# Softmax times V: normalising bank by bank, with half of the last head's first bank on ScalarE and the very last store in three parts

## Chip, cores, metric

One core of a Trainium2 chip runs the whole problem as one program. The metric is the device time of one execution in microseconds (us); lower is better. All runs quoted here, the profiled ones too, are marked as fast in the record. A profile shows one run, and not always a median one: that of three_only took 1064.35 us (median 1064.08), that of bank_three 1064.14 (1063.76).

## The reference

```python
# scores: 8 x 12 x 1024 x 1024 fp32, v: 8 x 12 x 1024 x 64 fp32
def reference(scores, v):
    scores_max = np.max(scores, axis=-1, keepdims=True)
    attn = np.exp(scores - scores_max)
    attn = attn / (np.sum(attn, axis=-1, keepdims=True) + 1e-8)
    return np.matmul(attn, v).astype(np.float32)
```

There are 96 heads. The kernel reads 402.65 MB of scores, 25.17 MB of v, and writes 25.17 MB: 453 MB in all. It leaves the maximum out, takes the exponential, multiplies by v with a column of ones beside it, and divides by the sum that this column gives.

## The kernel before

A loop of 24 iterations takes a group of four heads (k = 0 to 3) each. A head is 8 blocks of 128 query rows (r = 0 to 7), here called rows. For each row ScalarE takes the exponential (two rows at once, except at a group's end), PE transposes the 128x1024 block in 8 matmuls, VectorE copies the result from PSUM to SBUF, and PE multiplies it in 8 matmuls, three rows behind (LAG). Four rows' products of 65 columns share one PSUM bank, so a head has bank 0 (rows 0 to 3) and bank 1.

```python
    # heads(n0): one group; 4 heads of 8 rows
            for r in range(R):
                ...                                   # exp -> p_nat (ScalarE)
                for c in range(C):
                    turned = nc.tensor.transpose(out=psT[:, c * P : (c + 1) * P], ...)
                    in_line(turned)
                copy = nc.vector.tensor_copy(out=pt[:], in_=psT[:])
                ...
                if k == AHEAD - 1 and r == R - 1:
                    normalise(k, st, 0, 1, copy)      # bank 0 of the last head
                ...
                pending.append((n0, k, r, pt, st))
                if len(pending) > LAG:
                    finish(pending.pop(0))            # 8 products of an earlier row
```

Even heads keep both banks in one tile and are normalised in one go at their end; odd heads are normalised bank by bank. W is 64, T is 2: one normalisation is a reciprocal and two products, one for each half t of the partitions.

```python
    psO_whole = ps_pool.tile([P, R // G, 512], FP32, name="psO_whole")
    psO_banks = buffers(ps_pool, R // G, [P, 1, 512], FP32, "psO")
    ...
    def normalise(k, st, first, last, behind=None):
        psO = psO_whole if k % 2 == 0 else psO_banks[first]
        ...
        inverse = nc.vector.reciprocal(out=recip, in_=psO[:, :, :, D : D + 1])
        for t in range(T):
            ...
            nc.vector.tensor_tensor(out=rows..., in0=psO[part, :, :, 0:D],
                                    in1=recip[part].to_broadcast(...), op=mult)
```

Two heads share an output tile and are stored together, 512 KB at a time. The very last store is cut in two by t. All loads and stores stand in one queue, issued by SyncE (SP).

The softmax here doesn't subtract the row's maximum and nothing guards it: scores larger than these inputs give would overflow.

Of the kernel before, what the change touches and what calls it, by code (L numbers as in the profile page):

```python
# [8 lines left out]
FP32 = mybir.dt.float32  # L9
# [5 lines left out]
def kernel(  # L15
# [6 lines left out]
    nc = tc.nc  # L22
    P = 128

    B, H, SQ, SK = scores.shape
    Bv, Hv, SKv, D = v.shape
# [3 lines left out]
    R = SQ // P  # L30
    C = SK // P
    M = D + 1
    EB = 2
    G = 4
    LAG = 3
    AHEAD = 4
# [3 lines left out]
    T = 2  # L40
# [10 lines left out]
    W = P // T  # L51
    out_bh = out.rearrange("b h (j x) d -> (b h j) (x d)", j=W)
# [3 lines left out]
    ps_pool = ctx.enter_context(tc.tile_pool(name="pspool", bufs=1, space=bass.MemoryType.PSUM))  # L56
# [6 lines left out]
        out=order16[:].rearrange("p (t j) -> p t j", t=T),  # L63
        in_=ident32[:].rearrange("p (j t) -> p t j", t=T),
# [3 lines left out]
    vones_bufs = []  # L68
# [7 lines left out]
    def buffers(pool, count, shape, dtype, name):  # L76
        return [pool.tile(shape, dtype, name=f"{name}{k}") for k in range(count)]
# [5 lines left out]
    out_bufs = buffers(sb_pool, 2, [P, T, R, D], FP32, "out_sb")  # L83
# [1 line left out]
    psT_bufs = buffers(ps_pool, 4, [P, SK], FP16, "psT")  # L85


    psO_whole = ps_pool.tile([P, R // G, 512], FP32, name="psO_whole")
    psO_banks = buffers(ps_pool, R // G, [P, 1, 512], FP32, "psO")
    turn = {}  # L90

    def take(bufs):
        k = turn.get(id(bufs), 0)
        turn[id(bufs)] = k + 1
        return bufs[k % len(bufs)]
# [5 lines left out]
    def after(a, b):  # L101

        tc.add_manual_dep(
            a.ins,
            b.ins.name,
            mybir.DependencyInfo(mybir.DependencyClass.NoSync, mybir.DependencyReason.DATA),
            reason="order",
        )

    def in_line(op):  # L110

        if line:
            after(op, line[-1])
        line.append(op)

    def queue(dma):

        if queued:
            after(dma, queued[-1])
        queued.append(dma)  # L120
# [1 line left out]
    def one(bh, n):  # L122
        return bh[bass.ds(n, 1)].rearrange("o p r d -> (o p) r d")

    def normalise(k, st, first, last, behind=None):

        psO = psO_whole if k % 2 == 0 else psO_banks[first]
        psO = psO[:, :, 0 : G * M].rearrange("p b (g m) -> p b g m", m=M)
        recip = st["recip"][:, first:last]
        inverse = nc.vector.reciprocal(out=recip, in_=psO[:, :, :, D : D + 1])  # L130
        if behind is not None:
            after(inverse, behind)
        h = k % T
        for t in range(T):
            part = slice(t * W, (t + 1) * W)
            rows = st["out_sb"][h * W : (h + 1) * W, t, first * G : last * G, :]
            nc.vector.tensor_tensor(  # L137
                out=rows.rearrange("j (b g) d -> j b g d", g=G),
                in0=psO[part, :, :, 0:D],
                in1=recip[part].to_broadcast([W, last - first, G, D]),  # L140
                op=mybir.AluOpType.mult,
            )

    def finish(u):

        n0, k, r, pt, st = u
        b, g = r // G, r % G
        if r == 0:
            st["recip"] = take(rc_bufs)
            st["out_sb"] = out_bufs[k // T]  # L150
        bank = psO_whole[:, b] if k % 2 == 0 else psO_banks[b][:, 0]
        for c in range(C):
            product = nc.tensor.matmul(  # L153
                out=bank[:, g * M : (g + 1) * M],
                lhsT=pt[:, c * P : (c + 1) * P],
                rhs=st["vones"][:, c, 0:M],
                start=(c == 0),
                stop=(c == C - 1),
            )
            in_line(product)  # L160
        if k % 2 == 1:
            if g == G - 1 and (b > 0 or k < AHEAD - 1):
                normalise(k, st, b, b + 1)
        elif r == R - 1:
            normalise(k, st, 0, R // G)
        if r == R - 1:
            spread_v(k)
            if k == T - 1:
                store(n0, 0)

    def store(n0, k, parts=1):

        rows = out_bh.rearrange("(m x) y -> m x y", x=P)
        size = T * R * D // parts
        for part in range(0, T * R * D, size):
            dma = nc.sync.dma_start(
                out=rows[bass.ds((n0 + k) // T, 1)].rearrange("o x y -> (o x) y")[
                    :, part : part + size
                ],
                in_=out_bufs[k // T][:].rearrange("x t r d -> x (t r d)")[:, part : part + size],  # L180
            )
            for other in stores:
                apart(dma, other)
                apart(other, dma)
            apart(dma, dma)
            stores.append(dma)
            queue(dma)
# [4 lines left out]
    def apart(a, b, reason="stores of two heads are disjoint"):  # L192
        tc.declare_no_dep(a.ins, b.ins, across_iterations=True, reason=reason)
# [11 lines left out]
    def load(k, n, parts=(R,), r=0, **cond):  # L205
        for rows in parts:
            queue(
                nc.sync.dma_start(  # L208
                    out=s_bufs[k][:, r : r + rows, :],
                    in_=one(sc_bh, n)[:, r : r + rows, :],  # L210
                    **cond,
                )
            )
            r += rows
# [11 lines left out]
    def spread_v(k):  # L226

        for s in range(S):
            nc.gpsimd.tensor_copy(  # L229
                out=vones_bufs[k][s * Q : (s + 1) * Q, :, 0:D].rearrange(  # L230
                    "i (h l) d -> i h l d", l=L
                ),
                in_=v_sb[k * Q : (k + 1) * Q, :, s],
            )
# [6 lines left out]
    def last(n0):  # L241


        before = queued[-1:]

        with tc.If(n0 < BH - 2 * AHEAD) as cmp:  # L246
            queued[:] = before
            load(AHEAD - 2, (n0 + (2 * AHEAD - 2)) % BH)
            load_v((n0 + 2 * AHEAD) % BH)
            load(AHEAD - 1, (n0 + (2 * AHEAD - 1)) % BH)  # L250
            store(n0, AHEAD - T)
        with cmp.Else():
            with tc.If(n0 < BH - AHEAD) as cmp2:
                queued[:] = before
                load(AHEAD - 2, BH - 2, (4, 4))
                load(AHEAD - 1, BH - 1, (3,))
                store(n0, AHEAD - T)
                load(AHEAD - 1, BH - 1, (2, 1, 1, 1), 3)
            with cmp2.Else():
                queued[:] = before  # L260
                store(n0, AHEAD - T, T)

    def heads(n0):

        for k in range(AHEAD):
            st = dict(vones=vones_bufs[k])
            for r in range(R):
                if r % EB == 0:
                    p_nat = take(p_bufs)
                    rows = 1 if k == AHEAD - 1 and r > 0 else EB  # L270
                    for g in range(0, EB, rows):
                        exp = nc.scalar.activation(  # L272
                            out=p_nat[:, g : g + rows, :].rearrange(
                                "p r (x v) -> p x r v", v=Q * L
                            ),
                            in_=s_bufs[k][:, r + g : r + g + rows, :].rearrange(
                                "p r (i x l) -> p x (r i) l", i=Q, l=L
                            ),
                            func=EXP,
                        )  # L280
                        rewrite(p_nat, exp)
                p_row = p_nat[:, r % EB, :].rearrange("p (h q l) -> p h l q", q=P, l=L)
                psT = take(psT_bufs)
                for c in range(C):
                    turned = nc.tensor.transpose(  # L285
                        out=psT[:, c * P : (c + 1) * P],
                        in_=p_row[:, c // L, c % L, :],
                        identity=order16[:],
                    )
                    in_line(turned)  # L290
                pt = take(pt_bufs)
                copy = nc.vector.tensor_copy(out=pt[:], in_=psT[:])  # L292
                rewrite(pt, copy)
                if k == AHEAD - 1 and r == R - 1:

                    normalise(k, st, 0, 1, copy)
                if r == R - 1:
                    load_next(k, n0)
                pending.append((n0, k, r, pt, st))
                if len(pending) > LAG:  # L300
                    finish(pending.pop(0))
        while pending:
            finish(pending.pop(0))
        last(n0)

    assert BH % AHEAD == 0 and BH >= 2 * AHEAD and SK == Q * S * C
# [40 lines left out]
```

## Time and profile before

| | |
|---|---|
| time, median of 3 (later of 6) runs | 1064.0 us (1063.86 to 1064.33) |
| span of the profiled run | 1061.8 us |
| DMA engines busy | full in 39 of 40 slices |
| last scores landed | 1052.04 |
| PE's last semaphore increment | 1056.61 |
| last store issued, landed | 1057.97, 1060.03 |

Times within a span count from its first instruction. A line of a timeline gives start, length, engine, line of the kernel, operation and tiles; x4 is a count of merged instructions, and the bracket has the engine's idle time before and what the profile takes for its end. In the lines VectorE is DVE, ScalarE is ACT, GpSimd is POOL, PE's weight loads are PEld, and SPq is the queue that SyncE issues transfers to. The entry on what ended the idle time is inferred: where an instruction waits for several semaphores it can be wrong. I also used the trace's own records of semaphore updates and DMA landings, which have no view of their own here; numbers from them are given in plain text. An "increment" below is one such update: PE adds one to its semaphore for every matmul and every weight load, and the other engines wait for its count.

The prediction below shows the page and the end of the span. These are ScalarE's instructions at the last boundary between two groups, in the kernel before:

```profile
1020.27 1.28 ACT L272 ACT_TABLE_LOAD   x1 [3.27 <-PE psO L153]
1021.57 3.71 ACT L272 ACTIVATE p_nat<-s_nat 128x2048 f16<-128x2048 f32 x2
```

ScalarE ends its exponentials of the group before at 1017.0. It then stands idle for 3.27 us, by the landing records not for PE but for the first head of the last group, which lands at 1020.19, loads its table and starts. PE and VectorE are then still busy with the last rows of the group before, PE until 1021.5 and VectorE until 1023.2: ScalarE runs ahead of them across the boundary.

### The profile page before, as it was taken

To read this page: it belongs to the slowest core of one execution; us is meant where nothing else is said; L and a number is where in the kernel's file an instruction comes from. 1 tells how busy PE (TensorE), PEld (TensorE's weight loads), DVE (VectorE), ACT (ScalarE), POOL (GpSimd) and SP (SyncE) were. 2 spreads that over 40 slices of the span, in tenths; PEclk is the share of its full clock that TensorE was granted. 3 is DMA by queue.
4 is the path that set the end of the run, shared out by engine and by line. 5 is a ranking of instruction groups with operands and counts; after the bars stand their busy time and mean duration, and the time that the engine had idled before them with its cause. 6 is when DMAs were issued, how large, how long until landed. Compare 5 with 4: busy or idle time off the path is not lost.

```text
span 1061.8 us, 32325 instructions
## 1 busy us (share of the span) xinstructions
PE 727.3 (68%) x12288; PEld 687.9 (65%) x12288; DVE 677.5 (64%) x1205; ACT 740.3 (70%) x480; POOL 244.3 (23%) x406
## 2 busy tenths in 40 slices
PE   2766766677666767667686775767767676666776
PEld 2766766667666667666676665667666675666665
DVE  1765665756666666666676665766657575676667
ACT  3766776666767668676685866767666677666686
POOL 3123211131121311212112221122211321213113
PEclk9887878978888788887888888977889788887889
DMA  9999999999999999999999999999999999999996
GB/s 396 433 413 433 435 435 433 433 433 432 426 430 433 435 433 435 433 435 424 429 433 435 435 432 434 423 442 423 432 435 432 435 425 443 435 425 430 431 434 267
DMA packets 25059, 453.05 MB, mean 427 GB/s; under 512 B 2784, under 2 KB 2784, under 8 KB 9440
## 3 DMA queue, kind: packets, MB, share of 16 engines
q1 hardware_dynamic: 25056, 453.00, 99.4%
q8 instruction: 3, 0.05, 0.0%
HBM read 436.21 MB, written 25.17 MB: 435 GB/s over the span
## 4 chain that ended last, share of the span: by engine, by line
DMA 61%; PEld 10%; PE 8%; ACT 6%; DVE 4%; issue 4%; POOL 3%; SPq 1%; POOLq 1%; ACTq 0%
DMA s_nat<-in_scores_dram 61%; ACT p_nat L272 6%; PEld L285 6%; DVE pt L292 4%; PEld L153 4%; PE psO L153 4%; PE psT L285 3%; POOL vones L229 3%; PE psO_whole L153 1%; SPq L220 1%; SPq L208 0%; POOLq L229 0%; POOLq L246 0%; POOLq L313 0%; POOLq L342 0%
## 5 line engine op out<-in xcount | busy, mean ns | idle before, releaser
L272 ACT ACTIVATE p_nat<-s_nat 128x2048 f16<-128x2048 f32 (+1 forms) x456 | 709.5, 1630 | 218.9 <-DMA s_nat<-in_scores_dram 191.2
L285 PE MATMUL psT<-order,p_nat 128*128 128x128 f16 x6144 | 572.1, 250 | 310.6 <-ACT p_nat L272 309.8
L292 DVE COPY pt<-psT 128x1024 f16<-128x1024 f16 x768 | 515.7, 688 | 366.7 <-PE L153 123.2
L285 PEld LDWEIGHTS <-p_nat 128*128 128x128 f16 x6144 | 457.6, 124 | 338.4 <-ACT p_nat L272 337.4
L229 POOL CAST vones<-v_sb 32x512 f16<-32x512 f32 x400 | 243.5, 609 | 814.5 <-PE L285 490.2
L153 PEld LDWEIGHTS <-pt 128*128 128x128 f16 x6144 | 300.9, 106 | 29.6 <-DVE pt L292 26.7
L153 PE MATMUL psO<-vones,pt 128*128 128x65 f16 x3072 | 175.7, 203 | 18.1 <-DVE pt L292 14.9
L153 PE MATMUL psO_whole<-vones,pt 128*128 128x65 f16 x3072 | 182.7, 207 | 0.0
L272 ACT ACT_TABLE_LOAD x24 | 30.8, 1283 | 94.1 <-PE psO L153 67.4
L137 DVE TENSOR_TENSOR out_sb<-psO,recip 64x256 f32<-64x256 f32 x192 | 81.2, 423 | 6.1
L137 DVE TENSOR_TENSOR out_sb<-psO_whole,recip 64x512 f32<-64x512 f32 x96 | 66.0, 688 | 3.0
L130 DVE RECIPROCAL recip<-psO 128x4 f32<-128x4 f32 x96 | 16.7, 174 | 3.2 <-PE psO L153 0.9
L130 DVE RECIPROCAL recip<-psO_whole 128x8 f32<-128x8 f32 x48 | 9.5, 197 | 0.0
L71 DVE MEMSET vones<- 128x16 f16 x4 | 0.2, 72 | 0.8 <-PEq L331 0.8
L62 DVE CAST order<-ident 128x128 f16<-128x128 f32 x1 | 0.2, 228 | 0.4 <-POOL ident masks.py:199 0.4
masks.py:199 POOL TENSOR_SCALAR_AFFINE_SELECT ident<-ident 128x128 f32<-128x128 f32 x1 | 0.3, 294 | 0.1
masks.py:197 POOL MEMSET ident<- 128x128 f32 x1 | 0.2, 206 | 0.3 <-POOLq L331 0.3
L331 POOL MEMSET const-float32-0.0<- 128x1 f32 x1 | 0.1, 98 | 0.3 <-issue 0.3
L331 POOL MEMSET const-bfloat16-1.0<- 128x1 bf16 x1 | 0.1, 101 | 0.0
L331 POOL MEMSET const-uint8-127<- 128x1 uint8 x1 | 0.1, 101 | 0.0
L331 POOL MEMSET const-float32-1.0<- 128x1 f32 x1 | 0.1, 98 | 0.0
## 6 DMA issues: line engine op xcount, KB each, us to landing
s_nat<-in_scores_dram SPq DMA_DIRECT2D x96, 4096.0 KB, 32.0
v_sb<-in_v_dram SPq DMA_DIRECT2D x24, 1024.0 KB, 18.6
out_dram<-out_sb SPq DMA_DIRECT2D x47, 512.0 KB, 26.1
s_nat<-in_scores_dram SPq DMA_DIRECT2D x2, 2048.0 KB, 31.7
s_nat<-in_scores_dram SPq DMA_DIRECT2D x1, 1536.0 KB, 32.2
s_nat<-in_scores_dram SPq DMA_DIRECT2D x3, 512.0 KB, 20.8
s_nat<-in_scores_dram SPq DMA_DIRECT2D x1, 1024.0 KB, 24.7
out_dram<-out_sb SPq DMA_DIRECT2D x2, 256.0 KB, 2.0
```

Of the source, the lines that this page charges most:

```text
L62: nc.vector.tensor_copy(out=order16[:].rearrange("p (t j) -> p t j", t=T), in_=ident32[:].rearrange("p (j t) -> p t j", t=T),)
L71: nc.vector.memset(vo[:, :, D : D + 2], 1.0)
L130: inverse = nc.vector.reciprocal(out=recip, in_=psO[:, :, :, D : D + 1])
L137: nc.vector.tensor_tensor(out=rows.rearrange("j (b g) d -> j b g d", g=G), in0=psO[part, :, :, 0:D], in1=recip[part].to_broadcast([W, last ...
L153: product = nc.tensor.matmul(out=bank[:, g * M : (g + 1) * M], lhsT=pt[:, c * P : (c + 1) * P], rhs=st["vones"][:, c, 0:M], start=(c == 0) ...
L220: nc.sync.dma_start(out=v_sb[:].rearrange("x h s l d -> x (h s l d)"), in_=rows[bass.ds(n // AHEAD, 1)].rearrange("o x y -> (o x) y"),)
L229: nc.gpsimd.tensor_copy(out=vones_bufs[k][s * Q : (s + 1) * Q, :, 0:D].rearrange("i (h l) d -> i h l d", l=L), in_=v_sb[k * Q : (k + 1) * ...
L272: exp = nc.scalar.activation(out=p_nat[:, g : g + rows, :].rearrange("p r (x v) -> p x r v", v=Q * L), in_=s_bufs[k][:, r + g : r + g + ro ...
L285: turned = nc.tensor.transpose(out=psT[:, c * P : (c + 1) * P], in_=p_row[:, c // L, c % L, :], identity=order16[:],)
L292: copy = nc.vector.tensor_copy(out=pt[:], in_=psT[:])
L331: nc = _bacc.Bacc("TRN2", target_bir_lowering=False, num_devices=1)
```

## The change

The intent: VectorE is busy almost without a gap at the very end, so take work from it there. Even heads are normalised bank by bank too, so that less stands ahead of the last copies; ScalarE takes one half of the last head's bank 0; and the last store goes in three parts, so that bank 0 leaves while bank 1 is still being made.

```diff
-    psO_whole = ps_pool.tile([P, R // G, 512], FP32, name="psO_whole")
-    psO_banks = buffers(ps_pool, R // G, [P, 1, 512], FP32, "psO")
+    psO_bufs = buffers(ps_pool, 2 * (R // G), [P, 512], FP32, "psO")
...
-    def normalise(k, st, first, last, behind=None):
+    def normalise(k, st, b, behind=None):
...
         for t in range(T):
             part = slice(t * W, (t + 1) * W)
+            if behind is not None and t == T - 1:
+                for g in range(G):
+                    nc.scalar.activation(
+                        out=st["out_sb"][h * W : (h + 1) * W, t, b * G + g, :],
+                        in_=psO[part, g, 0:D],
+                        func=mybir.ActivationFunctionType.Copy,
+                        scale=recip[part, g],
+                    )
+                continue
             nc.vector.tensor_tensor(
...
-        if k % 2 == 1:
-            if g == G - 1 and (b > 0 or k < AHEAD - 1):
-                normalise(k, st, b, b + 1)
-        elif r == R - 1:
-            normalise(k, st, 0, R // G)
+        if g == G - 1 and (b > 0 or k < AHEAD - 1):
+            normalise(k, st, b)
...
+        parts = [(slice(0, T), slice(0, R // G))]
+        if not whole:                                 # the very last store
+            parts = [(slice(0, T), slice(0, R // G - 1))]
+            parts += [(slice(t, t + 1), slice(R // G - 1, R // G)) for t in range(T)]
```

The loop's body is the same in every iteration, so ScalarE's four activations stand at the end of every group, not of the last alone.

More of the change, by code (lines that the diff above doesn't have):

```diff
@@ L123, in one @@
         return bh[bass.ds(n, 1)].rearrange("o p r d -> (o p) r d")
-    def normalise(k, st, first, last, behind=None):
-        psO = psO_whole if k % 2 == 0 else psO_banks[first]
-        psO = psO[:, :, 0 : G * M].rearrange("p b (g m) -> p b g m", m=M)
-        recip = st["recip"][:, first:last]
-        inverse = nc.vector.reciprocal(out=recip, in_=psO[:, :, :, D : D + 1])
+    def normalise(k, st, b, behind=None):
+        psO = st["psO"][b][:, 0 : G * M].rearrange("p (g m) -> p g m", m=M)
+        recip = st["recip"][:, b]
+        inverse = nc.vector.reciprocal(out=recip, in_=psO[:, :, D : D + 1])
         if behind is not None:
@@ L135, in normalise @@
             part = slice(t * W, (t + 1) * W)
-            rows = st["out_sb"][h * W : (h + 1) * W, t, first * G : last * G, :]
+            if behind is not None and t == T - 1:
[7 more added lines that the diff above has]
+                continue
             nc.vector.tensor_tensor(
-                out=rows.rearrange("j (b g) d -> j b g d", g=G),
-                in0=psO[part, :, :, 0:D],
-                in1=recip[part].to_broadcast([W, last - first, G, D]),
+                out=st["out_sb"][h * W : (h + 1) * W, t, b * G : (b + 1) * G, :],
+                in0=psO[part, :, 0:D],
+                in1=recip[part].to_broadcast([W, G, D]),
                 op=mybir.AluOpType.mult,
@@ L150, in finish @@
             st["out_sb"] = out_bufs[k // T]
-        bank = psO_whole[:, b] if k % 2 == 0 else psO_banks[b][:, 0]
+        bank = st["psO"][b]
         for c in range(C):
@@ L169, in finish, with store @@
                 store(n0, 0)
-    def store(n0, k, parts=1):
-        rows = out_bh.rearrange("(m x) y -> m x y", x=P)
-        size = T * R * D // parts
-        for part in range(0, T * R * D, size):
-            dma = nc.sync.dma_start(
-                out=rows[bass.ds((n0 + k) // T, 1)].rearrange("o x y -> (o x) y")[
-                    :, part : part + size
-                ],
-                in_=out_bufs[k // T][:].rearrange("x t r d -> x (t r d)")[:, part : part + size],
-            )
+    def store(n0, k, whole=True):
+        to = out_bh.rearrange("(m x) y -> m x y", x=P)[bass.ds((n0 + k) // T, 1)]
+        to = to.rearrange("o x (t b y) -> (o x) t b y", t=T, b=R // G)
+        of = out_bufs[k // T][:].rearrange("x t (b g) d -> x t b (g d)", g=G)
+        parts = [(slice(0, T), slice(0, R // G))]
+        if not whole:
+            parts = [(slice(0, T), slice(0, R // G - 1))]
+            parts += [(slice(t, t + 1), slice(R // G - 1, R // G)) for t in range(T)]
+        for t, b in parts:
+            dma = nc.sync.dma_start(out=to[:, t, b, :], in_=of[:, t, b, :])
             for other in stores:
@@ L260, in last @@
                 queued[:] = before
-                store(n0, AHEAD - T, T)
+                store(n0, AHEAD - T, whole=False)
     def heads(n0):
         for k in range(AHEAD):
-            st = dict(vones=vones_bufs[k])
+            st = dict(vones=vones_bufs[k], psO=[take(psO_bufs) for b in range(R // G)])
             for r in range(R):
@@ L294, in heads @@
                 if k == AHEAD - 1 and r == R - 1:
-                    normalise(k, st, 0, 1, copy)
+                    normalise(k, st, 0, copy)
                 if r == R - 1:
```

## The prediction

> **What bounds the kernel now.** I read the page's time slices first, because they say whether there is one limit or several stages.
>
> ```profile
> span 1061.8 us, 32325 instructions
> DMA  9999999999999999999999999999999999999996
> GB/s 396 433 413 433 435 435 433 433 433 432 426 430 433 435 433 435 433 435 424 429 433 435 435 432 434 423 442 423 432 435 432 435 425 443 435 425 430 431 434 267
> ```
>
> The DMA engines are full in 39 of 40 slices; only the last (26.5 us) falls off. The DMA line of the page gives 453.05 MB; at the 432 GB/s of the stretch from 44 to 1049 us that is 1049 us of the 1061.8. No engine is over 70% busy. So nothing that only makes DVE, ScalarE or PE busier or idler inside the loop can move the time; what can move is the tail after the last data. I therefore read the busy table by window, in four cuts of the end.
>
> ```profile
> core 0: us, PE busy (x) PEld busy (x) DVE busy (x) ACT busy (x) POOL busy (x), PEclk, DMA share, GB/s
> 44.00:1049.00 1005.00, 702.19 (x11877) 664.89 (x11873) 652.97 (x1158) 712.82 (x463) 228.95 (x376) 0.83 1.01 432
> 1049.00:1052.10 3.10, 2.38 (x44) 2.14 (x45) 2.65 (x5) 3.10 (x4) 1.46 (x3) 1.00 0.26 104
> 1052.10:1058.10 6.00, 3.38 (x65) 2.64 (x62) 5.32 (x12) 1.24 (x2) 2.19 (x5) 0.92 0.21 87
> 1058.10:1060.10 2.00, 0.00 (x0) 0.00 (x0) 0.00 (x0) 0.00 (x0) 1.22 (x2) 0.50 0.68 262
> ```
>
> The table's last two cuts show where the change can work: DVE is 5.32 of 6.00 us busy, and then two microseconds hold nothing but the last stores. (POOL's casts there are for a head that never comes.) The third view is the timeline of that end, engine by engine; "x4" counts merged instructions, brackets hold the idle time before and its releaser.
>
> ```profile
> 1049.91 0.69 DVE L292 COPY pt<-psT 128x1024 f16<-128x1024 f16 x1 [0.27 <-PE L285]
> 1050.52 0.20 DVE L130 RECIPROCAL recip<-psO_whole 128x8 f32<-128x8 f32 x1
> 1050.88 0.69 DVE L292 COPY pt<-psT 128x1024 f16<-128x1024 f16 x1 [0.15 <-PE psT L285]
> 1051.60 1.41 DVE L137 TENSOR_TENSOR out_sb<-psO_whole,recip 64x512 f32<-64x512 f32 x2
> 1053.04 2.48 DVE L292 COPY pt<-psT 128x1024 f16<-128x1024 f16 x4
> 1055.44 0.17 DVE L130 RECIPROCAL recip<-psO 128x4 f32<-128x4 f32 x1
> 1055.64 0.88 DVE L137 TENSOR_TENSOR out_sb<-psO,recip 64x256 f32<-64x256 f32 x2
> 1056.63 0.18 DVE L130 RECIPROCAL recip<-psO 128x4 f32<-128x4 f32 x1
> 1056.85 0.88 DVE L137 TENSOR_TENSOR out_sb<-psO,recip 64x256 f32<-64x256 f32 x2
> ...
> 1055.58 0.43 PE L153 MATMUL psO<-vones,pt 128*128 128x65 f16 x8 [0.17 <-DVE pt L292]
> ...
> 1057.30 0.36 SPq L176 DMA_DIRECT2D out_dram<-out_sb  x1
> ...
> 1057.97 0.33 SPq L176 DMA_DIRECT2D out_dram<-out_sb  x1
> ```
>
> At first sight DVE is the bound from 1050.88 to 1056.52: head 2's whole-tile normalisation (1.41) stands ahead of the last four copies. But the last reciprocal does not start at 1056.52, when DVE is free, nor at 1056.01, when the last PE row (1055.58 + 0.43) is over; it starts at 1056.63. I looked at the trace's records of PE's semaphore increments: PE posts one for every matmul and every weight load (2 x 12288), and from 1032.19 to 1056.611 there are 815 of them exactly 0.030 us apart without one gap. The last, at 1056.611, releases the reciprocal 0.02 later. One row needs 32 (8 transposes, 8 products, each with its load), so 0.96 us: that is the spacing of the copies from 1047.03 to 1050.88, each with 0.27 idle. So in the tail **PE's stream of increments is the pacemaker**, DVE comes just behind it, and the end is: last increment, reciprocal 0.18, two products 0.88, last store issued at 1057.97, landed at 1060.03 (2.05 later), closing barrier to 1061.8.
>
> **What the Trainium skill says.** "TensorE: Matmul & The Clock Gate", The cost: per-tile semaphore tail: increments of matmuls serialise, with 26.3 ns for each. The trace agrees in kind, with 30 ns. [...]The trace: 2.02 and 2.05 us for 256 KB, 2.64 for the 512 KB store at 1052.16, so [...]bytes cost about 0.6 us for each 256 KB. "ScalarE: Activation LUTs", Table sets: copy is in every set. The instruction order agrees: one table load an iteration in both kernels.
>
> **The change part by part.**
> *Even heads bank by bank.* Before, a reciprocal of 8 columns (197 ns) and two 64x512 products (688): 1.57 us. After, two reciprocals of 4 (174) and four 64x256 (423): 2.04. DVE gains 0.47 x 48 heads = 22 us, all under a full DMA: no time. In the tail it moves head 2's bank 0 to before 1049, where copies have 0.27 idle each; of the 1.41 at 1051.60, 0.88 remains. By DVE alone the copies of rows 4 to 7 could start from 1052.51 instead of 1053.04, a gain of 0.53. But the increments that release them arrive, counted back from the end, at 1051.84, 1052.80, 1053.76 and 1054.72: the last copy can start at 1054.75 instead of 1054.84. It gains 0.09, and the final increment nothing: it stays at 1056.61.
> *First bank of the last head, half by ScalarE.* It takes 0.44 off DVE between 1055.44 and 1056.52. DVE was done 0.11 before the wait for PE ended, so it gains nothing on the path. Its cost: four 64x64 activations. From exp at 1024 (1.04 us) and 2048 (1.90) columns: 0.83 ns a column and 0.19 fixed, hence 0.24 each, and since the instruction order shows each waiting for the one before, some 0.28 to 0.30: about 1.15 us from 1055.55, done near 1056.7. Inside the loop they stand ahead of the next table load, which waits for the next head's data anyway (1020.19 in the last boundary), and ScalarE then has another 1.07 idle at 1029.96.
> *The last store.* Before two of 256 KB, in halves by t; after, bank 0 whole (256 KB), then two of 128 KB. The queue needs 0.68 from one issue to the next (57.30 to 57.97). The first can go at about 56.7, the second at max(57.30, 56.7+0.68 = 57.38), the third at about 58.0 to 58.1, no earlier than now. But its packets are half the size: the trace has 8 packets an engine at 80 ns for 2 KB (155 for 4 KB), so 1 KB should take some 42: 0.34 instead of 0.64, a gain of 0.30. The closing waits, 0.066 apart, are one shorter after that landing: 0.07.
> Sum: 0 (loop) + 0 (DVE relief) - 0.37 (third store) + 0.1 (ScalarE pushing the issues) = **-0.3 us**: 1064.0 - 0.3 = **1063.7**.
>
> **The rivals.**
> *DVE relief counts in full.* If the increments were only a record and the copies really queued on DVE, the tail would gain 0.53 and, with ScalarE's half, reach bank 1 sooner: about 0.8 with the store, 1063.2. For it: DVE has no gap from 1050.88 to 1056.52. Against: the last reciprocal and POOL's cast at 1056.76 both start behind the last increment and 0.6 behind the last matmul.
> *ScalarE becomes the wait.* If each activation takes 0.4, the first store goes at 1057.2, the third at 1058.55: the gain turns into +0.2, 1064.2. For it: four dependent small instructions, and the queue issues in order. Against: the fitted 0.24.
> *More DVE work delays copies.* If the added 0.47 a head isn't absorbed by the 0.27 gaps around 1047, rows 4 to 7 start late and PE's stream gets a gap: up to +0.5, 1064.5. Against: by my schedule the backlog is gone by row 2.
> *Transfers starve in the loop.* The store of heads 2 and 3 waits for ScalarE too and stands in one queue with loads. But a load lands 32.0 us after its issue and moves in about 9.7 (4.19 MB at 432 GB/s): three loads are queued, and a delay of 1 us is hidden. The whole stores keep their 4 KB rows, so DMA efficiency is untouched.
>
> **Range and chances.** The three runs of before spread 0.47 us, as much as the effect. The rivals run from 1063.2 to 1064.5, the dearer one unlikely. Predicted 1063.7, range 1063.1 to 1064.3. 2% is 21 us: only a broken overlap of the loop could reach it, and no view hints at one. Faster 0.005, same 0.985, slower 0.01.
>
> **What would show it.** DVE busy 677.5 + 22.6 - 24 x 0.423 = about 690 us (ScalarE takes one 64x256 in each of 24 iterations), ScalarE 740 + 96 x 0.24 = about 763; DMA slices unchanged. In the tail: the copies of rows 4 to 7 spread out (about 1052.5, 1053.1, 1053.8, 1054.75 on the old scale) instead of in one block, and yet the last reciprocal at the same distance from the last landing of scores as before (1052.04 to 1056.63, 4.6 us); four activations of about 0.24; the third store issued near 1058.0 and landed in some 1.7 us. It is wrong if the last reciprocal comes 0.3 or more earlier (the increments aren't the pacemaker), if the third issue comes after 1058.3 (ScalarE), or if DMA's share drops before the last slice.

## The result

The changed kernel took **1066.81 us** (median of 6 runs, 1066.44 to 1067.35) against 1064.02 of the kernel before in the same rounds. The ratio is 1.0027, with a 95% interval of 1.0014 to 1.0040. Ratios here are the mean time of one kernel's fast runs over that of the other's of the same rounds, so not quite the ratio of the medians. Within 2% it counts as the same, but it is 2.8 us slower and outside the predicted range of 1063.1 to 1064.3.

The page of the changed kernel, first line and the two lines on the DMA engines and on ScalarE's new instructions:

```profile
span 1064.8 us, 32854 instructions
DMA  9999999999999999999999999999999999999995
L137 ACT ACTIVATE out_sb<-psO,recip 64x64 f32<-64x64 f32 x96 | 22.0, 303 | 105.9 <-PE psO L160 105.9
```

The DMA engines are as full as before, and the last scores land at 1052.15, 0.1 later than before. So nearly all of the 3.0 us of the span appear behind the last data. They are not all made there: the prediction looked for what can move only in the tail, and most of the loss begins at the last boundary between groups, some 30 us earlier. In front of those 96 small activations ScalarE waits 105.9 us in all, 4.4 an iteration. That is the new wait. ScalarE at the last boundary, in the changed kernel:

```profile
1021.29 0.92 ACT L137 ACTIVATE out_sb<-psO,recip 64x64 f32<-64x64 f32 x4 [4.10 <-PE psO L160]
1022.73 1.28 ACT L276 ACT_TABLE_LOAD   x1 [0.52 <-issue]
1024.03 1.91 ACT L276 ACTIVATE p_nat<-s_nat 128x2048 f16<-128x2048 f32 x1
```

Against the two lines of before: the exponentials of the last group start at 1024.03 instead of 1021.57, 2.46 later, though their data landed at about the same time (1020.40, and 1020.19 in the kernel before). ScalarE no longer runs ahead; its four activations need the reciprocal of the head that VectorE is just finishing. And they don't start with the reciprocal (over at 1020.59) but behind VectorE's own half of the bank (over at 1021.04): in the changed program ScalarE's wait is for one increment of VectorE more than the reciprocal's, and the trace has this wait end at 1021.09.

What that does to PE shows in the busy table by window: us, then busy time of PE, PEld, VectorE, ScalarE and GpSimd with counts, then the granted PE clock, the DMA share and GB/s. First before, then after.

```profile
1023.00:1026.00 3.00, 2.47 (x23) 2.30 (x24) 1.41 (x3) 3.00 (x3) 1.72 (x3) 0.51 1.01 437
1026.00:1029.00 3.00, 2.80 (x53) 2.58 (x52) 2.24 (x5) 2.89 (x2) 0.00 (x0) 0.93 0.88 371
1029.00:1032.00 3.00, 1.61 (x33) 1.49 (x34) 1.98 (x3) 2.04 (x2) 0.00 (x0) 1.00 1.00 426
```

```profile
1023.00:1026.00 3.00, 0.01 (x1) 0.01 (x1) 0.00 (x0) 2.99 (x3) 1.36 (x3) 0.50 1.06 459
1026.00:1029.00 3.00, 3.00 (x28) 2.83 (x29) 1.50 (x3) 3.00 (x2) 0.00 (x0) 0.50 0.88 371
1029.00:1032.00 3.00, 3.00 (x43) 3.00 (x42) 1.96 (x3) 3.00 (x3) 0.00 (x0) 0.56 0.96 410
```

By 1032, in the kernel before, PE has done 109 matmuls of the last group, and it has idled for 1.4 us of the last stretch, waiting for the second head's data. In the changed kernel it has done 72, without any idle time in the last two stretches, at half the clock. From here on PE is a stream of 30 ns increments without a gap in both kernels, so the lag stays. From the records:

| | before | after | difference |
|---|---|---|---|
| first increment of the last group | 1023.65 | 1026.12 | +2.46 |
| increments until the last slow one | 51 in 2.94 us | 117 in 5.65 us | +0.73 over 30 ns each |
| waits for the second head's data | 0.85 | 0 | -0.85 |
| last increment of all | 1056.61 | 1058.95 | **+2.34** |

Both kernels have the same 1024 increments in this group (32 a row), so a late start comes out at the end unless a wait in between takes it up. ScalarE itself made its delay good: its last exponential starts at 1052.32, and at 1052.30 in the kernel before. PE did not, because the 0.85 us of the table were all the slack that it had.

The end, in the changed kernel: VectorE, ScalarE and the issues of the three stores.

```profile
1057.66 0.17 DVE L128 RECIPROCAL recip<-psO 128x4 f32<-128x4 f32 x1
1057.87 0.42 DVE L144 TENSOR_TENSOR out_sb<-psO,recip 64x256 f32<-64x256 f32 x1
1058.98 0.18 DVE L128 RECIPROCAL recip<-psO 128x4 f32<-128x4 f32 x1 [0.69 <-PE psO L160]
1059.19 0.88 DVE L144 TENSOR_TENSOR out_sb<-psO,recip 64x256 f32<-64x256 f32 x2
...
1058.54 0.92 ACT L137 ACTIVATE out_sb<-psO,recip 64x64 f32<-64x64 f32 x4 [5.18 <-PE psO L160]
...
1059.48 0.71 SPq L185 DMA_DIRECT2D out_dram<-out_sb  x1
1060.52 0.37 SPq L185 DMA_DIRECT2D out_dram<-out_sb  x1
1061.20 0.33 SPq L185 DMA_DIRECT2D out_dram<-out_sb  x1
```

VectorE is idle for 0.69 us before the last reciprocal, waiting for PE: the work that was taken from it was not what held the end. ScalarE is done with bank 0 at 1059.46, and only then goes the first store, which moreover takes 0.71 us to issue instead of 0.36 (it has 256 rows of 1 KB, not 128 of 2 KB). The third store leaves 2.25 us after PE's last increment; in the kernel before, the second and last left 1.36 after it. The whole of it: +2.34 (PE) + 0.89 (issue of the last store) - 0.20 (it lands in 1.85 instead of 2.05) - 0.07 (the closing barrier) = +2.96, and the spans differ by 3.0.

### The profile page after: what moved, and what is told of

Read it like the earlier page. It is cut to its first block, busy times and chain, and to the rows that moved or that the text cites. A ratio compares the mean times of both kernels' runs of the same rounds, so it can differ in the third digit from the quotient of the medians.

```text
span 1064.8 us, 32854 instructions
## 1 busy us (share of the span) xinstructions
PE 714.9 (67%) x12288; PEld 678.6 (64%) x12288; DVE 690.1 (65%) x1325; ACT 760.2 (71%) x576; POOL 244.6 (23%) x406
## 4 chain that ended last, share of the span: by engine, by line
DMA 61%; PE 11%; PEld 9%; DVE 5%; ACT 5%; issue 3%; POOL 3%; SPq 1%; POOLq 1%; ACTq 0%; PEldq 0%
DMA s_nat<-in_scores_dram 61%; PE psT L289 6%; PE psO L160 5%; PEld L289 5%; DVE pt L296 5%; ACT p_nat L276 5%; PEld L160 4%; POOL vones L233 3%; SPq L224 1%; SPq L212 0%; POOLq L233 0%; POOLq L250 0%; POOLq L317 0%; POOLq L346 0%; ACTq L276 0%
## 5 line engine op out<-in xcount | busy, mean ns | idle before, releaser
L289 PE MATMUL psT<-order,p_nat 128*128 128x128 f16 x6144 | 563.2, 248 | 320.6 <-ACT p_nat L276 319.5
L289 PEld LDWEIGHTS <-p_nat 128*128 128x128 f16 x6144 | 452.0, 124 | 346.2 <-ACT p_nat L276 344.9
L160 PE MATMUL psO<-vones,pt 128*128 128x65 f16 x6144 | 354.1, 203 | 22.7 <-DVE pt L296 21.6
L160 PEld LDWEIGHTS <-pt 128*128 128x128 f16 x6144 | 296.5, 105 | 33.3 <-DVE pt L296 29.3
L144 DVE TENSOR_TENSOR out_sb<-psO,recip 64x256 f32<-64x256 f32 x360 | 151.9, 422 | 70.0 <-DMA out_dram<-out_sb 58.8
L137 ACT ACTIVATE out_sb<-psO,recip 64x64 f32<-64x64 f32 x96 | 22.0, 303 | 105.9 <-PE psO L160 105.9
L128 DVE RECIPROCAL recip<-psO 128x4 f32<-128x4 f32 x192 | 33.4, 174 | 16.5 <-PE psO L160 16.5
```

Source lines behind the costliest of these rows:

```text
L128: inverse = nc.vector.reciprocal(out=recip, in_=psO[:, :, D : D + 1])
L137: nc.scalar.activation(out=st["out_sb"][h * W : (h + 1) * W, t, b * G + g, :], in_=psO[part, g, 0:D], func=mybir.ActivationFunctionType.Co ...
L144: nc.vector.tensor_tensor(out=st["out_sb"][h * W : (h + 1) * W, t, b * G : (b + 1) * G, :], in0=psO[part, :, 0:D], in1=recip[part].to_broa ...
L160: product = nc.tensor.matmul(out=bank[:, g * M : (g + 1) * M], lhsT=pt[:, c * P : (c + 1) * P], rhs=st["vones"][:, c, 0:M], start=(c == 0) ...
```

## The experiments

All were timed in five rounds; "before" is the kernel before in the same rounds. The table has the medians and, from each profiled run, the start of the last table load, PE's last increment and the issue of the last store by SP.

| run | us | before | ratio | table load | last increment | last store |
|---|---|---|---|---|---|---|
| (before) | 1064.02 | | | 1020.27 | 1056.61 | 1057.97 |
| (changed) | 1066.81 | 1064.02 | 1.0027 | 1022.73 | 1058.95 | 1061.20 |
| bank_only | 1063.95 | 1063.95 | 1.0000 | 1020.30 | 1056.63 | 1057.99 |
| scalar_only | 1066.32 | 1063.95 | 1.0023 | 1023.22 | 1059.00 | 1060.47 |
| three_only | 1064.08 | 1063.95 | 1.0001 | 1020.81 | 1057.16 | 1058.82 |
| scalar_no_wait | 1063.64 | 1063.95 | 0.9997 | 1020.46 | 1056.80 | 1058.17 |
| busy_scalar | 1067.01 | 1063.94 | 1.0028 | 1023.70 | 1059.93 | 1061.29 |
| scalar_first | 1067.20 | 1063.93 | 1.0029 | 1022.91 | 1059.02 | 1061.96 |
| fewer_products | 1062.98 | 1063.93 | 0.9992 | 1020.52 | 1055.61 | 1057.41 |
| bank_three | 1063.76 | 1063.93 | 0.9999 | 1020.73 | 1057.07 | 1058.62 |
| split_second | 1064.45 | 1063.94 | 1.0005 | 1021.32 | 1057.28 | 1058.82 |
| split_two_queues | 1064.10 | 1063.94 | 1.0003 | 1021.30 | 1057.11 | 1057.97 |
| split_loads | 1140.46 | 1063.93 | 1.0721 | | | |
| early_table | 1071.40 | 1064.00 | 1.0070 | 1024.85 | 1064.38 | 1065.92 |

In split_two_queues the last part went by ScalarE's queue, so 1057.97 is SP's second part. Where the ratio is below 1.001 the 95% interval contains 1, so by it such a run is not told from the kernel before; the intervals of all the others do not contain 1.

### One part of the change at a time

**bank_only**: the change without ScalarE's part, and with the store in two halves.

```diff
-            if behind is not None and t == T - 1:
-                for g in range(G):
-                    nc.scalar.activation(...)
-                continue
...
-                store(n0, AHEAD - T, whole=False)
+                store(n0, AHEAD - T, T)               # two halves, as before
```

> The first part of the change alone: every head is normalised bank by bank by VectorE, the last store stays in two halves, ScalarE has nothing to do with it. My theory after seeing the result (ScalarE's half is what costs): as before, 1064.0 within 0.4 us, ScalarE's last table load near 1020.3 us and PE's last increment near 1056.6 us from the start of the span. Rival A (the 22 us more of VectorE work, or VectorE's new wait for the landing of the last iteration's store, 58.8 us in all, is what costs): about 1066 us or more, with the last increment 2 us later.

```profile
1020.30 1.28 ACT L266 ACT_TABLE_LOAD   x1 [3.31 <-PE psO L150]
...
1056.65 0.18 DVE L128 RECIPROCAL recip<-psO 128x4 f32<-128x4 f32 x1 [0.23 <-PE psO L150]
```

No difference at all: 1063.95 and 1063.95. Rival A falls. It also confirms a step of the prediction: VectorE has less ahead of the last copies and now idles 0.23 us ahead of the last reciprocal, which yet starts at 1056.65, against 1056.63 in the kernel before. What VectorE is spared at the end buys nothing.

**scalar_only**: the kernel before with ScalarE's part.

```diff
+            if behind is not None and t == T - 1:
+                for g in range(G):
+                    nc.scalar.activation(
+                        out=rows[:, g, :], in_=psO[part, 0, g, 0:D],
+                        func=mybir.ActivationFunctionType.Copy, scale=recip[part, 0, g],
+                    )
+                continue
```

> The second part alone: the kernel before, but half of the last head's first bank is normalised by ScalarE, and the last store stays in two halves. My theory: ScalarE can no longer run ahead of the last rows of a head into the next group of heads; its last table load moves from 1020.3 to about 1022.7, PE's last increment from 1056.6 to about 1058.9 us, and the time rises by some 2.3 us to about 1066.3. Rival A: 1064.0, as VectorE does less, not more. Rival B (the three stores cost it): 1064.0.

```profile
1021.78 0.91 ACT L139 ACTIVATE out_sb<-psO,recip 64x64 f32<-64x64 f32 x4 [4.76 <-PE psO L162]
1023.22 1.28 ACT L281 ACT_TABLE_LOAD   x1 [0.53 <-issue]
```

+2.4 us, with the table load and the last increment where they were expected, or a little later. This part alone carries 2.4 of the 2.8 us.

**three_only**: the kernel before with the new store function.

> The third part alone: the kernel before, with the very last store in three parts (bank 0 of both halves, then bank 1 of each half). My theory: the first part needs 0.71 instead of 0.36 us to issue, but it may go at about 1056.5, before the last increment matters, so the third goes near 1058.3 instead of 1057.97 and lands in 1.85 instead of 2.05 us: 1064.1, within 0.4 of before. Rival B (the queue's three issues are the main cost): 1065 to 1067 us.

+0.13 us, not resolved from zero. The third store went at 1058.82 and not near 1058.3, but 0.53 of that is the later start of the last group in the profiled run (table load at 1020.81). From PE's last increment to the last landing it is 3.52 us (1060.68 - 1057.16) against 3.42 before: the shorter last transfer is eaten up by one more issue. Rival B falls as the main cause. The change as a whole is some 0.5 us beyond scalar_only. By the lines of the end above, that is where the two parts meet: the first of the three stores waits for ScalarE, takes 0.71 to issue, and the other two stand behind it. No run tests this sum by itself.

### The wait, or the work?

**scalar_no_wait**: the changed kernel, but ScalarE's four activations read an SBUF tile written long ago, not the bank and the reciprocals. Its output is wrong, which doesn't matter for the time.

```diff
-                        in_=psO[part, g, 0:D],
-                        func=mybir.ActivationFunctionType.Copy,
-                        scale=recip[part, g],
+                        in_=st["vones"][part, g, 0:D],
+                        func=mybir.ActivationFunctionType.Copy,
```

> The changed kernel, but ScalarE's four small activations read a tile in SBUF that has long been written, and not the reciprocals and the PSUM bank (the result is wrong on purpose in those elements). ScalarE does the same number of instructions of the same size at the same place, without the wait for VectorE. My theory (the wait in ScalarE's order costs, not the work): the four run right behind the last exponential at about 1017 to 1018, the last table load is back at about 1020.3, PE's last increment at about 1056.6, and the time within 0.5 us of before, some 2.5 us below the changed kernel. Rival C (the four activations' own time, about 1 us an iteration, is what costs): it stays at 1066 or more.

```profile
1017.24 0.69 ACT L137 ACTIVATE out_sb<-vones 64x64 f32<-64x64 f16 x4
1020.46 1.28 ACT L275 ACT_TABLE_LOAD   x1 [2.53 <-PE psO L159]
```

The same number of instructions in the same place, but the last table load is back at 1020.46 and the time at 1063.64, 3.2 us below the changed kernel. (They read SBUF and not PSUM and are 0.17 instead of 0.23 us each; that is not where 3 us are.) So the wait costs, not the work.

**busy_scalar**: the opposite test. The kernel before, where six useless activations keep ScalarE from the boundary, without any link to VectorE.

```diff
+                if k == AHEAD - 1 and r == R - 1:
+                    for _ in range(6):
+                        nc.scalar.activation(out=idle_sb[:], in_=p_nat[:, r % EB, :], func=Copy)
```

> The kernel before, with six useless activations of 128x1024 (into a tile that nobody reads) behind the last exponential of each group of four heads. They wait for nothing of VectorE or PE's products and change no other engine's work; they only keep ScalarE from reaching the next group's table load before about 1022.7 to 1023.5 us, as the wait does in the changed kernel. My theory (whatever holds the last table load back moves PE's last increment by the same time less what little slack there is): the last table load moves by 2.4 to 3.2 us, PE's last increment by about as much (2.2 to 3.1), and the time rises to 1066.2 to 1067.1 us. Rival (it is the traffic between VectorE and ScalarE on the last bank, not the table load's place, that costs): 1064.0 within 0.4.

```profile
1017.18 6.50 ACT L285 ACTIVATE idle<-p_nat 128x1024 f16<-128x1024 f16 x6
1023.70 1.28 ACT L273 ACT_TABLE_LOAD   x1
```

The table load moves by 3.43 us (2.4 to 3.2 expected) and PE's last increment by 3.32; the time rises by 3.1. Nothing else in the kernel was touched. Whatever holds ScalarE back at the last boundary comes out at the end, nearly whole. In the 22 boundaries before it, the same delay costs nothing: 6 us of ScalarE in each iteration would be over 130 us otherwise.

**scalar_first**: the two halves of the bank in the other order in the program.

```diff
-        for t in range(T):
+        for t in reversed(range(T)):
```

> The changed kernel with the two halves of a bank taken in the other order in the program: ScalarE's activations stand ahead of VectorE's product. In the changed kernel's program ScalarE waits for one increment of VectorE more than the reciprocal's, that is, for VectorE's product too, so the halves run one after the other. My theory: the wait shrinks by the product's 0.42 us; the last table load goes from 1022.7 to about 1022.3, PE's last increment from 1058.95 to about 1058.5, and ScalarE's part is done about 0.4 earlier once more against that increment: 1065.9 to 1066.2 us, still about 2 us above before. Rival (the order of the halves is the main cost): within 0.5 us of before.

A miss: 1067.20, not 1066. ScalarE does start right behind the reciprocal at the end (1058.15 against a reciprocal over at 1057.90). But VectorE's product of bank 0 now waits for ScalarE, and the scheduler has put it behind the first product of bank 1, so the first store leaves at 1060.26 instead of 1059.48. At the boundary nothing is won, because in this run VectorE's reciprocal itself came 0.63 us later (1021.05 instead of 1020.42); why, I didn't find out. What stays of it: in whichever order they stand, the two engines' halves of this bank are done one after the other. Whether it is the common PSUM bank or the common output tile that makes the framework order them, no run here tells.

### Is PE's stream of increments really the pacemaker?

**fewer_products**: the kernel before with 6 instead of 8 products a row. Its output is wrong, which doesn't matter for the time.

```diff
-        for c in range(C):
+        for c in range(C - 2):
...
-                stop=(c == C - 1),
+                stop=(c == C - 3),
```

> The kernel before with 6 instead of 8 product matmuls for each row (the result is wrong on purpose). A row then has 28 increments of PE instead of 32: 0.84 us instead of 0.96 at 30 ns. My theory (PE's increments pace the tail): PE's stream is no longer behind ScalarE's exponentials (0.91 us a row), it has gaps, and the last reciprocal comes 1 to 1.6 us earlier: 1062.4 to 1063.0 us. Rival (VectorE's copies and products pace the tail): VectorE has the same work, so 1064.0 within 0.3.

```profile
1045.40 4.51 DVE L292 COPY pt<-psT 128x1024 f16<-128x1024 f16 x7
1050.39 0.69 DVE L292 COPY pt<-psT 128x1024 f16<-128x1024 f16 x1 [0.38 <-PE psO L153]
...
1055.16 0.88 DVE L137 TENSOR_TENSOR out_sb<-psO,recip 64x256 f32<-64x256 f32 x2
1056.07 0.18 DVE L130 RECIPROCAL recip<-psO 128x4 f32<-128x4 f32 x1
```

The stream now has gaps, the copies follow each other at 0.64 us instead of 0.96, and the last reciprocal comes at 1056.07 instead of 1056.63; the time falls by 0.95 us. The 95% interval (0.9978 to 1.0005) just contains 1, though the slowest of the five runs (1063.44) is below the fastest of the kernel before (1063.71). The direction is as expected, the size at the low end. The lines show why: the reciprocal now stands directly behind VectorE's product (1055.16 + 0.88 = 1056.04). VectorE is the next pacemaker, only 0.6 us behind. One caution: PE also has less arithmetic here, so this run does not separate its increments from its matmuls. That they are separate is seen in the kernel before, where the last matmul is over at 1056.01 and its increment comes at 1056.61.

### A faster version?

**bank_three**: the change without ScalarE's part.

> The change without ScalarE's part: bank by bank and the three stores. My theory: PE's last increment at 1056.6; the first store goes at about 1056.45 behind VectorE's two products of bank 0 and takes 0.71 to issue, the third goes at about 1058.2 and lands 1.85 later: 1063.7 to 1064.0 us. Rival (the three stores cost by themselves, the 0.4 us that the changed kernel has beyond the second part alone): 1064.3 or more.

1063.76 us, 0.17 below before, by the interval (0.9985 to 1.0013) not told from it. Its first and third store went at 1056.89 and 1058.62, each some 0.4 later than expected, as the last group started 0.46 later in the profiled run. Of the correct versions it has the lowest median, by less than the noise. It is the changed kernel without its loss, and little more.

**split_loads**: bank_three, with the first two heads of a group each loaded in two halves of four rows.

```diff
-            load(k, (n0 + (AHEAD + k)) % BH, cond=n0 < BH - AHEAD)
+            load(k, (n0 + (AHEAD + k)) % BH, (R // 2, R // 2), cond=n0 < BH - AHEAD)
```

> A try at a faster version: the one without ScalarE's part, with the loads of the first two heads of a group in two halves of four rows, so that ScalarE and PE can start on half a head. My theory (the end is the start of PE's last group of rows plus 1024 increments of 30 ns, unless data are later): at the last boundary ScalarE starts about 2 to 3 us earlier, PE does not stand idle from 1022.1 to 1023.7 and 1031.3 to 1032.0, and the end comes about 1 us earlier, then set by the last rows' landing: 1062.5 to 1063.2 us. Rival (the end is set by the last landing and what follows it, as the full DMA queue suggests): no change from the version without ScalarE's part.

A clear failure: 1140 us. The framework gives the transfers eight semaphores in turn. A group now has nine transfers. The ninth, a store, gets the semaphore of the first, and the first load of the next group can't be issued before that store has landed: one such store is issued at 720.49 and lands at 752.80, and SP's wait ends at 752.82. SP's own waits say how long in all:

```profile
SPq L202 <- DMA out_dram<-out_sb: 492.7, 24, 22.0
```

493 us in 24 waits in front of loads: the queue that should hold three loads runs dry.

**split_second**: the same with the second head alone, which makes eight transfers with eight semaphores.

```diff
+            load(k, ..., (R // 2, R // 2) if k == 1 else (R,), cond=n0 < BH - AHEAD)
```

> The version without ScalarE's part, with only the second head of a group loaded in two halves of four rows. That is one more transfer a group and, by the program, no transfer then waits for the landing of one issued in the same group, which is what went wrong with two split heads. Theory: PE's gap of some 0.8 us before 1032 us, a wait for the whole of the second head of the last group, goes, and the 1024 increments run on from there: 1062.8 to 1063.3 us. Rival (PE's stream is not what sets the end): 1063.8, as without the split.

1064.45: no gain, and a miss (1062.8 to 1063.3 expected). From the table load to PE's last increment it is 35.96 us instead of 36.34, so the gap that was aimed at did shrink by 0.4. But the last scores land at 1052.97, where the other runs without an extra transfer in the loop have 1051.9 to 1052.5: the 23 more transfers seem to cost the bound itself more than they give back. This rests on one profile of each run.

**split_two_queues**: split_second, with the last part of the last store issued by ScalarE.

```diff
+            queue_of = nc.scalar if t.start == T - 1 else nc.sync
-            dma = nc.sync.dma_start(out=to[:, t, b, :], in_=of[:, t, b, :])
+            dma = queue_of.dma_start(out=to[:, t, b, :], in_=of[:, t, b, :])
```

> As the one with the second head split, and the third part of the last store is issued by ScalarE, which has nothing left to do then, so that it need not stand 0.68 us behind the second in the sync queue. Theory: the third part is issued within 0.1 us of VectorE's last product instead of about 0.4 after it: another 0.3 us less, 1062.5 to 1063.0. Rival (landing of the earlier parts or the closing waits set the end): same as with one queue.

1064.10, where 1062.5 to 1063.0 was expected. The third part did go where it should, at 1058.26, 0.04 behind VectorE's last product. But from the last increment to the end of the span it is 5.19 us, 5.23 with one queue. A gain is not resolved.

**early_table**: split_second with an exponential of one column ahead of each group, so that the table is loaded before the data land.

> The version without ScalarE's part and with the second head split, with an exponential of one column ahead of each group, so that the table load (1.28 us) no longer waits for the first head of the group to land. Theory: in the last group the first exponential starts about 1.28 us earlier after its data, and as PE's increments run on without a gap from there, the last one comes 1.0 to 1.3 us earlier than with the second head split alone: 1063.1 to 1063.5 us against 1064.45. Rival (something later, such as the landing of the last rows, sets the end): 1064.2 or more.

A failure: 1071.40. The last scores land at 1060.55, 7.6 us later than in split_second, and the transfers are behind all along the loop (the store that lands at 901.05 there lands at 906.96 here). The part aimed at did what it should: the last group's first exponential starts 0.10 us behind its data (1028.21 and 1028.11), 1.39 in split_second. That the transfers are slower shows in their landings. Each posts sixteen of them; up to 410 us the last comes at most 0.04 us behind the fifteenth, and from there the distance grows with every group, to 3.57 at the end (never over 0.09 in split_second). So one sixteenth of every transfer falls ever further behind. Packets of 8 KB also take 314 ns instead of 309. Why, stays open; the engine that issues them has no new wait that I could find.

## Why the prediction was wrong

What held:

- Up to the last boundary the loop is bound by DMA and hides what was added: DMA's slices are as before, VectorE's busy time rose to 690.1 us (690 predicted), ScalarE's to 760.2 (763).
- Sparing VectorE at the end is worth nothing, as PE's increments pace it: shown by bank_only, whose last copies also start where the prediction put them (1052.52 and 1054.73; 1052.51 and 1054.75 predicted).
- The third store lands sooner, in 1.85 us, a gain of 0.20 where 0.30 was predicted. Its 1 KB packets take 46 ns (42 predicted), and those of 2 KB took 84 in the kernel before, not the 80 that the prediction read.
- The activations' own time: 0.92 us for four (about 1.15 predicted).

The step that failed is this one, in the part on ScalarE: "Inside the loop they stand ahead of the next table load, which waits for the next head's data anyway (1020.19 in the last boundary), and ScalarE then has another 1.07 idle at 1029.96." In the sum it is the term "0 (loop)"; what it stood for measured +2.34 us. It has two errors.

First, when the four are done. I took them to start right behind the reciprocal and never read that reciprocal's time at the last boundary. It was at 1020.89 in the kernel before, already behind the landing at 1020.19, so the four could not be hidden by it. In the changed kernel they ran from 1021.29 to 1022.21.

Second, whose idle time it is. ScalarE's 1.07 us did absorb its delay, and its later 0.99 the rest: ScalarE is on time for its last five rows. But I had said earlier in the same prediction that PE's stream of increments runs without a gap from 1032.19 to the end, and so has nothing to absorb a late start with. All its slack was the 0.85 us in front of that stretch. The prediction named the pacemaker and then measured the slack of another engine. busy_scalar shows the pass-through: 3.43 us in, 3.32 out. In the changed kernel it was 2.46 in, 2.34 out, as the table of increments has it. One of the prediction's own signs shows it too: the last reciprocal was to come 4.6 us after the last landing of scores, and came after 6.83 (1052.15 to 1058.98).

A smaller error sits in the stores. "The first can go at about 56.7" left out that ScalarE waits for VectorE's half too (0.42 us), that its two waits stand in series (0.24 us from that half's end to the first activation), and that 256 rows take 0.71 us to issue: relative to PE's last increment the last issue came 0.89 later than before, not 0.1. The stores' terms of the sum, -0.37 and +0.1, measured -0.27 and +0.89. The third issue came at 1061.20, past the prediction's own mark of 1058.3. None of the rivals had the cause: "ScalarE becomes the wait" looked for it at the end of the span alone, and made it 0.2 us.

The cold clock's share, 0.73 of the 2.34 us, is worked out from the records and was not tested by itself. One kept trace bears on it: in scalar_only PE's first increment of the last group comes 0.48 later than in the changed kernel, but the clock is full again 4.1 us after the first matmul instead of 5.7, and the last increment is only 0.04 later. So this share is partly luck: it depends on where the group's start falls among the clock's changes, which lie 3.41 us or a multiple of it apart in the records of these runs. "TensorE: Matmul & The Clock Gate", What's actually happening, has PE's clock at half after an idle window of about 3.4 us and full again after about 3.4 us of work, with free-running windows. The trace agrees on half and full clock (0.50 and 1.00); it took 2.9 us of work to recover in the kernel before and 5.7 in the changed one. It does not agree on the idle time: the record goes to half at 1023.03 in the kernel before and at 1021.41 in the changed one, when PE has had no matmul for 1.6 and 0.4 us.

## What to carry to other kernels

An in-order engine that runs ahead of the others across a loop boundary is worth more than its busy time tells: a small piece of work that needs the slow engine's last result stops it there, and in a loop body it does so in every iteration. When a delay is said to be absorbed, look for the slack on the engine that sets the end, not on the one that is delayed. And before work is taken from an engine that has no gaps, check which event its last instruction really starts with.

## What the Trainium skill lacked or had wrong

- "TensorE: Matmul & The Clock Gate", The cost: per-tile semaphore tail, treats the increments as a tail behind one packed group (26.3 ns each). Here they were 30 ns each, weight loads counted too, and a lasting limit: 815 in 24.4 us without a gap, 0.96 us a row, until the last came 0.60 us behind the last matmul's end, which the profile models.
- "ScalarE: Activation LUTs", What ACT_TABLE_LOAD costs, adds a drain of about 1.38 us to the load's 1.283 at a switch to a different set. It says nothing of a load without a switch, which is what these are as far as the program shows: it uses exp and copy alone. The load is 1.283 here in both kernels, the next exponential starts 0.01 us behind it (1021.557 to 1021.568), and in busy_scalar it starts 0.02 behind the activation before it; no drain of that length stands on either side.
- "DMA: Bandwidth & Descriptors" does not say how the time to issue a store from SyncE's queue grows with its rows: 0.71 us for 256 KB as 256 rows of 1 KB, 0.36 for 256 KB as 128 rows of 2 KB, 0.33 to 0.37 for 128 KB as 128 rows of 1 KB.
- No page that I read says that more transfers than semaphores in a loop body make the issuing engine wait for landings: 493 us in 24 waits when two transfers were added to seven and eight semaphores served them in turn.
